# Decoder step on one core: gates computed in pairs of blocks with seven products, kept in DRAM

## The chip, the cores and the metric

The kernel runs on one core of a Trainium2 chip. The metric is the time of one execution on the device in microseconds; a time given for a kernel is the median of several executions. TensorE is called PE, VectorE DVE, ScalarE ACT, GpSimd POOL and SyncE SP. SP computes nothing here; it issues most of the DMAs, in a fixed order.

## What is computed

One layer of a hybrid decoder, for 1024 prompt positions and 8 sample rows, 1032 columns in all, everything in fp32. A projection of the input feeds three branches (window attention, a diagonal state-space layer with GELU and GLU, and a spatial gating over chunks of 128 positions) and, for every branch, a gate per output channel:

```python
q, k, v, z_a, u_b, z_b, u_c, v_c, z_c, g = jnp.split(x @ w_in, cuts, axis=-1)
y_a, y_b, y_c = attention(q, k, v), glu(gelu(s5(u_b))), sgu(u_c, v_c)
ys = stack([y_a * silu(z_a), y_b * silu(z_b), y_c * silu(z_c)])    # 512 wide each
branch = einsum('ntbw,bwd->ntbd', ys, w_read)                      # to 1024, per branch
gates = sigmoid(g.reshape(n, t, 3, 1024))
merged = (gates * branch).sum(axis=2)
x = layernorm(ALPHA * x + merged @ w_o, ln_g, ln_b)
```

The gate projection, 1024 input channels to 3 x 1024 gate channels, is the largest single product. It is made in 24 blocks of 128 output channels, 8 for each branch.

## The kernel before

Everything is held transposed: channels on the 128 partitions, the 1032 columns along the free axis, in three chunks of 344 (`CW`). An fp32 product is made of three: each operand is split into a high part, rounded to a shorter format, and the remainder, and `mm3` (L98) adds high by high (L101), high by low (L102) and low by high (L103) in PSUM. A piece of 128 x 128 weights by 344 columns thus takes three matmuls, each with a weight load of its own.

Weights come in granules of 128 x 512 (`gran`, L136): a DMA on SP into a raw tile `wr` (4 buffers), the high part `wh` by ACT (L133), the low part `wl` by a subtraction (L134), on DVE in the first part of the program and on POOL from L812 on. A block of the input projection has 8 pieces of 128 input channels in two granules, hence 72 matmuls: 8 x 3 for each of three chunks. A readout block has 4 pieces in one granule and 36 matmuls.

The instruction order on each engine is set by a scheduler that simulates the program when it is built; `tc.high_priority()` lets a step go ahead, `pin` and `behind` fix an order. PSUM is given out in banks: three of the kind `mm`, four `ms`, one `mt`. Large SBUF tiles (`b2`, 128 x 2064, named `b` in the trace) are 21.

The stages behind the state-space layer:

- Attention in 8 blocks (`attn_block`, L743): scores, softmax on DVE and ACT, transposes of the probabilities (L788) and the output matmuls (L794). Its end (L799 to L803) multiplies by the gate path z and splits the result into `yah` and `yal`, in SBUF. The twelve projections of the gating branch (L814 to L829) are interleaved with it.
- `readout(b, ...)` (L837) for the branches b = 0, 1, 2, with eight blocks d each. For each it first projects the gate block with 72 matmuls on the columns of x, takes a tanh on ACT (L846), then makes the readout product with 36 matmuls. DVE multiplies it by the gate (L856 for b = 0, L859 else). For b = 1 POOL adds it to the sum (L861); for b = 2 DVE adds it (L863) and the sum is split for the output projection (L866 on ACT, L867 on DVE).
- GELU of the state-space result (L885) runs in four steps between the blocks of readout 0; its split stays in SBUF. GLU follows (four blocks of 36 matmuls). The spatial gating (`sgu_chunk`, L977; LayerNorm in L938 to L946, the gating itself at L990 to L993) runs between the blocks of readout 1. Its result goes through DRAM (`ycD`) and is read back and split (L1004 and L1005) before readout 2.
- The output projection and the LayerNorm close the program.

Of the kernel before, what the change touches and what calls it, by code (L numbers as in the profile page):

```python
# [11 lines left out]
F32 = mybir.dt.float32  # L12
# [4 lines left out]
OP = mybir.AluOpType  # L17
# [47 lines left out]
def decoder_step(ctx, tc, io):  # L65
# [65 lines left out]
    def split_w(src, hi, lo):  # L131
        with tc.high_priority():
            S.activation(hi, src, AF.Copy)  # L133
            lo_eng[0].tensor_tensor(lo, src, f(hi), op=OP.subtract)  # L134

    def gran(idx, pinned=False):  # L136
        raw = wp.tile([128, 512], F32, tag="wr", name=nm("wr"), bufs=4)
        i1 = nc.sync.dma_start(raw, io["wg"][idx])
        if pinned:
            behind(i1, xlast[0])  # L140
        hi = wp.tile([128, 512], F32R, tag="wh", name=nm("wh"), bufs=4)
        lo = wp.tile([128, 512], F32R, tag="wl", name=nm("wl"), bufs=4)
        split_w(raw, hi, lo)
        return hi, lo
# [24 lines left out]
    wz = cst.tile([128, 512], BF16, name="wz")  # L169
    V.memset(wz, 0.0)  # L170
# [3 lines left out]
    prm = b2()  # L174
# [206 lines left out]
    qD, zaD, zbD, uszD, vcD, ycD, pD = (spill(n_) for n_ in ("qD", "zaD", "zbD", "uszD", "vcD", "ycD", "pD"))  # L381
# [293 lines left out]
    yah = [b2(F32R) for _ in range(2)]  # L675
    yal = [b2(F32R) for _ in range(2)]

# [46 lines left out]
    for j in range(2):  # L724
        h3 = v2(yah[j][:, 0:2 * T], T)[:, :, 0:NS]
        V.tensor_copy(h3, ysm3[:, 2 * j:2 * j + 2])
        V.tensor_tensor(v2(yal[j][:, 0:2 * T], T)[:, :, 0:NS], ysm3[:, 2 * j:2 * j + 2], f(h3), op=OP.subtract)
# [15 lines left out]
    def attn_block(m):  # L743
# [52 lines left out]
        y3 = z4  # L796
        for j in range(2):
            js = slice(2 * j, 2 * j + 2)
            V.scalar_tensor_tensor(y3[:, js], v2(o, 128)[:, js], 0.5, z4[:, js],  # L799
                                   op0=OP.mult, op1=OP.mult)  # L800
            h3 = v2(yah[j][:, 0:2 * T], T)[:, :, q0:q0 + 128]
            S.activation(h3, y3[:, js], AF.Copy)  # L802
            V.tensor_tensor(v2(yal[j][:, 0:2 * T], T)[:, :, q0:q0 + 128], y3[:, js], f(h3), op=OP.subtract)  # L803
# [29 lines left out]

    macc = [b2() for _ in range(4)]
# [43 lines left out]
    def gelu_load(q):  # L878
        wa = wks[q % 2][:, 0:T]
        i1 = nc.sync.dma_start(v2(wa[:, NS:T], 256), ytd[q])  # L880
        if q == 0:
            pin(i1)
# [318 lines left out]
```

## Time and profile before

| | |
|---|---|
| median of 3 runs | 997.93 us (997.4 to 998.44) |
| the profiled execution | 1001.31 us |
| its span (first to last instruction) | 999.2 us |
| mean granted clock of PE | 0.995 of full |
| DMA | 103.40 MB, mean 103 GB/s |

The profile's page comes from one execution, which was 3.4 us longer than the median; 2.1 us of it lie outside the span. An engine's busy time is the union of its instructions' spans. A line such as `L103 PE MATMUL mm<-b,wl 128*128 128x344` is a group: line 103, a matmul with 128 x 128 weights and 344 columns into a bank `mm`, from an SBUF tile and a low weight part. In groups the last columns are busy time and mean duration (ns), and the idle time of the engine just before them with what ended it. PEclk is the granted clock as a share of full speed.

### The profile page before, as it was taken

The page shows a single profiled execution, that of the slowest core. Times are in us where ns is not written, and L with a number is a line of the kernel's source. Part 1 is how long each engine was busy: PE and PEld are TensorE (multiplying, and loading weights), DVE is VectorE, ACT ScalarE, POOL GpSimd, SP SyncE. Part 2 cuts the span into 40 slices and gives each one's busy share as a digit, 9 for nine tenths or more (in the row PEclk, how much of TensorE's full clock was granted, in tenths as well). Part 3 has the DMA queues.
Part 4 walks back from the last instruction along what each step waited for, and adds up shares of the span by engine and source line. Part 5 has one row for each costly group of instructions (what it writes and reads, how often), then busy time and mean ns, then how long its engine had stood idle before and what let it go on. Part 6 is the DMA issues. An engine that isn't in the chain of part 4 may idle for free.

```text
span 999.2 us, 15902 instructions
## 1 busy us (share of the span) xinstructions
PE 984.8 (99%) x6105; PEld 929.1 (93%) x6105; DVE 558.2 (56%) x1218; ACT 336.0 (34%) x764; POOL 210.4 (21%) x194
## 2 busy tenths in 40 slices
PE   9999999999999999998999999999999999999997
PEld 7999999999999988885999999999999999986886
DVE  5877599999966664453434125145531323245754
ACT  5312464434324555455424134111122222241000
POOL 0420000001311212111222222434543222201411
PEclk9999999999999999998999999999999999999999
DMA  8445624443434222221433323233342111043311
GB/s 298 141 146 121 179 62 106 116 134 100 130 103 138 71 81 88 72 69 41 127 99 106 114 96 110 76 105 106 106 138 53 44 44 52 11 186 111 123 69 64
DMA packets 95772, 103.40 MB, mean 103 GB/s; under 512 B 36536, under 2 KB 70968, under 8 KB 94672
## 3 DMA queue, kind: packets, MB, share of 16 engines
q1 hardware_dynamic: 91184, 96.04, 32.2%
q10 hardware_dynamic: 4512, 6.34, 2.1%
q8 instruction: 48, 0.79, 0.3%
q14 instruction: 28, 0.23, 0.1%
HBM read 75.74 MB, written 26.29 MB: 102 GB/s over the span
## 4 chain that ended last, share of the span: by engine, by line
PE 92%; DVE 5%; DMA 1%; ACT 1%; issue 1%; SPq 0%; DVEq 0%; ACTq 0%
PE mm L101 26%; PE mm L103 26%; PE mm L102 26%; PE ms L794 2%; DVE b L254 2%; PE mt L788 1%; PE ms L102 1%; PE ms L767 1%; PE ms L103 1%; PE ms L101 1%; DMA b<-qD 1%; PE ms L1040 1%; PE ms L990 1%; PE ms L768 1%; DMA b<-xT 1%
## 5 line engine op out<-in xcount | busy, mean ns | idle before, releaser
L101 PE MATMUL mm<-b,wh 128*128 128x344 f32 x1584 | 508.4, 321 | 1.0 <-ACT b L802 1.0
L102 PE MATMUL mm<-b,wh 128*128 128x344 f32 x1584 | 507.0, 320 | 0.0
L103 PE MATMUL mm<-b,wl 128*128 128x344 f32 x1584 | 506.8, 320 | 0.0
L103 PEld LDWEIGHTS mm<-b,wl 128*128 128x128 f32 x1584 | 297.5, 188 | 3.7 <-issue 3.6
L101 PEld LDWEIGHTS mm<-b,wh 128*128 128x128 f32 x1584 | 297.5, 188 | 3.4 <-ACT b L802 2.4
L102 PEld LDWEIGHTS mm<-b,wh 128*128 128x128 f32 x1584 | 297.8, 188 | 1.7 <-issue 1.6
L134 POOL TENSOR_TENSOR wl<-wr,wh 128x512 fp32r<-128x512 f32 x100 | 138.9, 1392 | 592.5 <-ACT wh L133 554.9
L133 ACT ACTIVATE wh<-wr 128x512 fp32r<-128x512 f32 x136 | 85.6, 630 | 168.2 <-PE mm L102 129.1
L859 DVE SCALAR_TENSOR_TENSOR ct<-ct,mm 128x344 f32<-128x344 f32 x48 | 24.5, 510 | 123.7 <-PE mm L103 86.5
L846 ACT ACTIVATE ct<-mm 128x344 f32<-128x344 f32 x72 | 32.5, 451 | 116.8 <-PE mm L103 111.2
L254 DVE TENSOR_TENSOR b<-b 128x512 f32<-128x512 f32 (+6 forms) x93 | 53.9, 586 | 0.9
L101 PE MATMUL mm<-b,b 128*128 128x512 f32 (+1 forms) x136 | 51.9, 385 | 0.0
L102 PE MATMUL mm<-b,b 128*128 128x512 f32 (+1 forms) x136 | 51.4, 381 | 0.0
L103 PE MATMUL mm<-b,b 128*128 128x512 f32 (+1 forms) x136 | 51.4, 381 | 0.0
L856 DVE SCALAR_TENSOR_TENSOR b<-ct,mm 128x344 f32<-128x344 f32 x24 | 12.1, 511 | 64.7 <-PE mm L103 64.7
L254 DVE TENSOR_TENSOR b<-b,b 128x512 f32<-128x512 f32 (+5 forms) x96 | 44.8, 502 | 0.9
L771 DVE CUSTOM_DVE_ANT_0 b<-ms,b,sink 128x256 f32<-128x256 f32 (+1 forms) x64 | 26.2, 464 | 26.6 <-PE ms L768 26.5
L101 PEld LDWEIGHTS mm<-b,b 128*128 128x128 f32 x136 | 25.5, 188 | 7.5 <-ACT b L1045 0.8
L778 ACT ACTIVATE b<-b,stat 128x256 f32<-128x256 f32 (+1 forms) x64 | 30.9, 485 | 3.0 <-DVE stat L774 2.9
L134 DVE TENSOR_TENSOR wl<-wr,wh 128x512 fp32r<-128x512 f32 x36 | 24.6, 686 | 12.0 <-ACT wh L133 11.9
L102 PEld LDWEIGHTS mm<-b,b 128*128 128x128 f32 x136 | 25.5, 188 | 6.0 <-issue 0.8
L789 ACT ACTIVATE b<-mt 128x512 f32<-128x512 f32 x30 | 17.8, 593 | 39.0 <-PE mt L788 38.8
(233 smaller groups left out, 1087.4 us busy)
## 6 DMA issues: line engine op xcount, KB each, us to landing
wr<-wg SPq DMA_DIRECT2D x136, 256.0 KB, 2.9
b<-wo SPq DMA_DIRECT2D x4, 1024.0 KB, 9.0
b<-xp SPq DMA_DIRECT2D x8, 512.0 KB, 3.7
b<-xT SPq DMA_DIRECT2D x7, 516.0 KB, 6.7
yp<-b ACTq DMA_DIRECT2D x7, 512.0 KB, 2.6
zct<-b SPq DMA_DIRECT2D x5, 512.0 KB, 5.4
b<-zct SPq DMA_DIRECT2D x32, 80.0 KB, 2.6
utd<-b SPq DMA_DIRECT2D x4, 544.0 KB, 3.8
```

What stands on the lines that cost most here:

```text
L101: PE.matmul(out, ah, bh, start=start and i == 0, stop=False)
L102: PE.matmul(out, ah, bl, start=False, stop=False)
L103: PE.matmul(out, al, bh, start=False, stop=stop and i == n - 1)
L133: S.activation(hi, src, AF.Copy)
L134: lo_eng[0].tensor_tensor(lo, src, f(hi), op=OP.subtract)
L254: (eng or V).tensor_tensor(out, a, b, op=op)
L771: V.tensor_tensor_reduce(sc[:, h, lo:], p3[:, u, lo:], al3[:, h, lo:], SCALE, sink[:, h:h + 1], OP.add, OP.max, mx[:, h:h + 1])
L778: S.activation(sc[:, h, lo:], sc[:, h, lo:], AF.Exp, bias=nmx[:, h:h + 1], accum_out=den[:, h:h + 1])
L789: S.activation(pt[:, g, kb], tps, AF.Copy)
L794: PE.matmul(o[64 * g:64 * g + 64, :], vtok[:, m - 1 + kb, 64 * g:64 * g + 64], pt[:, g, kb], start=kb == kbs[0], stop=kb == kbs[-1])
L846: S.activation(tg, gps[c][:, :CW], AF.Tanh, scale=0.5)
L859: V.scalar_tensor_tensor(tt, tgs[c], 1.0, ps[:, :CW], op0=OP.add, op1=OP.mult)
```

## The change

The gate projection leaves the readouts. All 24 blocks are made in one stretch between the attention's last steps and GLU, their tanh is written to DRAM (`gD`), and a readout reads the gates of two blocks back with one DMA of 1 MB.

Two blocks (`gate_std`) are made as before, with 72 matmuls of 344 columns. The other 22 are made in 11 pairs (`gate_pair`). For a pair the weights are seen as a 2 x 2 matrix of granules (two output blocks by two halves of the input channels), and x as a 2 x 2 matrix of quarters (two halves of the input channels by two halves of the columns, 516 each). Eight products of such blocks would give the pair; Winograd's form of Strassen's scheme gives it with seven products of sums and differences. A product is made in two column pieces of 258 (`QT`), 4 x 3 matmuls each, hence 7 x 2 x 12 = 168 matmuls a pair. The four sums of x are made once, on POOL, and split on ACT and DVE; the four sums of weights are made for each pair on POOL; the products are added up on DVE (L919), which takes 14 additions of 128 x 258 a pair, seven `add` calls of two pieces. High and low parts of half of the weights are kept in columns of the split x that no product uses any more (`strips`).

Moved with it: the attention writes its result to `yaD` and no longer splits it; GELU writes its result to `y2D`; GELU and the spatial gating run between the pairs; `y_split` reads the three branch results back (L1043) and splits them on ACT and DVE just before GLU, readout 0 and readout 2. The tile for the first, idle matmuls lies in the parameter tile. There are five raw weight buffers in place of four.

```diff
-        y3 = z4
-        for j in range(2):
...
-            S.activation(h3, y3[:, js], AF.Copy)
-            V.tensor_tensor(v2(yal[j][:, 0:2 * T], T)[:, :, q0:q0 + 128], y3[:, js], f(h3), op=OP.subtract)
+        V.scalar_tensor_tensor(z4, v2(o, 128), 0.5, z4, op0=OP.mult, op1=OP.mult)
+        nc.sync.dma_start(yaD[:, :, q0:q0 + 128], z4)
...
+    def gate_std(i):
+        def go(c, ps):
+            tg = ct()
+            S.activation(tg, ps[:, :CW], AF.Tanh, scale=0.5)
+            nc.sync.dma_start(gD[i][:, cols[c]], tg)
+        proj(GG + i, go)
...
+        TT(f11, f12, f11, OP.subtract, G)
+        TT(f12, f22, f12, OP.subtract, G)
+        TT(f22, f22, f11, OP.subtract, G)
+        TT(f21, f21, f22, OP.subtract, G)
...
+            S.activation(h_[:, o], t_[:, o], AF.Copy)
+            TT(l_[:, o], t_[:, o], f(h_[:, o]), OP.subtract)
...
+        a11, a21 = wraw(i11)[0], wraw(i21)[0]
+        s3 = wraw()
+        TT(s3, a11, a21, OP.subtract, G)
...
+        def prod(w, n_):
+            ps = [bank()[:, :QT], bank(pk)[:, :QT]]
+            for c in range(2):
+                mm3(ps[c], [(w[0][:, k * 128:(k + 1) * 128], w[1][:, k * 128:(k + 1) * 128]) + bop(n_, k, c)
+                            for k in range(4)])
+            return ps
...
+        def add(o, a, b):
+            for c in range(2):
+                with tc.high_priority():
+                    V.tensor_tensor(o[c], a[c], b[c], op=OP.add)
...
+        ps = prod(w11, (0, 0))
...
+        add(u2, p1, prod(w2, 2))
+        add(c11, p1, prod(whl(a12, G), (1, 0)))
+        outs(0, 0, c11)
+        add(u3, u2, prod(whl(s3, V), 3))
+        ps = prod(whl(s1, V), 1)
+        add(p1, u3, ps)
+        outs(1, 1, p1)
+        add(u2, u2, ps)
+        add(u3, u3, prod(whl(a22, G), 4))
+        outs(1, 0, u3)
+        add(u2, u2, prod(whl(s4, V), (1, 1)))
+        outs(0, 1, u2)
...
+    todo = []
+    for q in range(4):
+        todo += [(gelu_step, q), (sgu_step, 2 * q), (sgu_step, 2 * q + 1)]
+    for n_ in range(NPR):
+        if n_:
+            gate_pair(NSTD + 2 * n_)
+        for fn, a_ in todo[12 * n_ // (NPR - 2):12 * (n_ + 1) // (NPR - 2)]:
+            fn(a_)
+    y2 = [y_split(y2D, j) for j in range(2)]
...
-            gg = [gran((GG + b * 8 + d) * 2), gran((GG + b * 8 + d) * 2 + 1)]
             gr = gran(GR_READ + b * 8 + d)
-            gps = [bank() for _ in range(NCH)]
-            tgs = []
-            for c in range(NCH):
-                proj_mm({c: gps[c]}, gg, [c])
-                tg = ct()
-                S.activation(tg, gps[c][:, :CW], AF.Tanh, scale=0.5)
-                tgs.append(tg)
+            if d % 2 == 0:
+                gt = b2()
+                nc.sync.dma_start(v2(gt[:, 0:2 * T], T), gD[b * 8 + d:b * 8 + d + 2].rearrange("d p t -> p d t"))
+            tgs = [gt[:, (d % 2) * T + c * CW:(d % 2) * T + (c + 1) * CW] for c in range(NCH)]
...
+    ya = [y_split(yaD, j) for j in range(2)]
+    readout(0, [y[0] for y in ya], [y[1] for y in ya])
+    readout(1, ybh, ybl)
+    yc = [y_split(ycD, j) for j in range(2)]
+    readout(2, [y[0] for y in yc], [y[1] for y in yc])
```

How the order of instructions changes is shown at three places; names carry the buffer's numbers, and "x4" stands for four instructions in a row.

PE at the end of the attention, before: from the last projection matmul (into `mm547`) to the first of readout 0 (into `mm548`), L788 transposes and L794 output matmuls of the last blocks.

```order
L103 MATMUL mm547_5146<-b308_3075,wl539_5048 128x344
L794 MATMUL ms379_3775<-b318_3132,b196_2140 64x512
L788 MATMUL mt382_3817<-ident_75,b317_3131 128x128 x4
L788 MATMUL mt383_3823<-ident_75,b317_3131 128x128 x4
L794 MATMUL ms388_3868<-b318_3132,b196_2140 64x512
L788 MATMUL mt386_3856<-ident_75,b317_3131 128x128 x4
L788 MATMUL mt387_3862<-ident_75,b317_3131 128x128 x4
L794 MATMUL ms388_3868<-b318_3132,b196_2140 64x512 x3
L101 MATMUL mm548_5160<-b307_3074,wh538_5047 128x344
```

The same place now: the last standard gate block (344 columns), then the first pair (258 columns, `mm563` and `mm565`), with the transposes (L792 now) and output matmuls (L798 now) of the last attention block further apart. First the switch from the standard block to the pair:

```order
L102 MATMUL mm543_5170<-b31_160,wh537_5110 128x344
L103 MATMUL mm543_5170<-b30_159,wl538_5111 128x344
L792 MATMUL mt379_3790<-ident_75,b313_3126 128x128 x4
L798 MATMUL ms384_3835<-b314_3127,b196_2142 64x512
L101 MATMUL mm563_5260<-b12_108 128x258
L102 MATMUL mm563_5260<-b13_109,b12_108 128x258
L101 MATMUL ms564_5261<-b12_108 128x258
L102 MATMUL ms564_5261<-b13_109,b12_108 128x258
```

The pair begins while the last attention block is still in its softmax. Fifteen rows further on, in the same product of the pair:

```order
L102 MATMUL mm563_5260<-b13_109,b12_108 128x258
L103 MATMUL mm563_5260<-b12_108,b13_109 128x258
L792 MATMUL mt382_3823<-ident_75,b313_3126 128x128 x4
L101 MATMUL mm563_5260<-b18_129,b12_108 128x258
L102 MATMUL mm563_5260<-b19_130,b12_108 128x258
L103 MATMUL mm563_5260<-b18_129,b13_109 128x258
```

So a group of transposes stands among matmuls that use only x, its sums and gate weights.

SP, in front of readout 0. Before, it holds weight loads there (`wr` from `wg`, L138 in `gran`) and the loads for GLU (`pD`), as between GELU and GLU here:

```order
L138 DMA wr679_6218<-wg 128x512
L138 DMA wr689_6280<-wg 128x512
L138 DMA wr698_6341<-wg 128x512
L913 DMA b682_6224<-pD_658 128x1032 x2
L138 DMA wr708_6403<-wg 128x512
L138 DMA wr724_6503<-wg 128x512
L138 DMA wr727_6509<-wg 128x512
```

Now, from the last of the gates' writes (L914) on: L1082 is a load for GLU, L1043 reads the attention's result back, L1104 reads gates back.

```order
L914 DMA gD_660<-b553_5238 128x258 x2
L1082 DMA b924_8409<-pD_659 128x1032 x2
L134 DMA wr983_8792<-wg 128x512
L134 DMA wr989_8840<-wg 128x512
L1043 DMA b944_8530<-yaD_656 128x2064
L134 DMA wr996_8890<-wg 128x512
L1043 DMA b947_8538<-yaD_656 128x2064
L134 DMA wr1002_8938<-wg 128x512
L1104 DMA b953_8552<-gD_660 128x2x1032
L1104 DMA b966_8650<-gD_660 128x2x1032
L134 DMA wr1012_8994<-wg 128x512
```

The reads of the attention's result and of the first gates stand behind weight loads of GLU and readout 0, each of which needs a free raw buffer.

DVE with a chunk of the spatial gating, before, in readout 1: LayerNorm (L941 to L946) and gating (L992, L993), between gate products (L859).

```order
L992 TENSOR_TENSOR b720_6471<-ms771_6833,b717_6464 128x512
L940 BN_STATS s6794_6995<-ms793_6990 128x6
L993 TENSOR_TENSOR b720_6471<-b720_6471 128x512
L941 BN_AGGR s6794_6995<-s6794_6995 128x2
L944 TENSOR_SCALAR b721_6472<-ms793_6990,s6794_6995 128x512
L945 TENSOR_TENSOR b721_6472<-b721_6472,b717_6464 128x512
L946 TENSOR_TENSOR b721_6472<-b721_6472,b717_6464 128x512
```

Now, in a pair: the same steps are L985 to L991, L1036 and L1037; between them stand the pair's additions from PSUM (L919) and weight splits (L146).

```order
L986 BN_AGGR s6618_5798<-s6618_5798 128x2
L919 TENSOR_TENSOR b553_5238<-b553_5238,mm631_5865 128x258
L989 TENSOR_SCALAR b584_5491<-mt617_5793,s6618_5798 128x512
L146 TENSOR_TENSOR b19_130<-wr654_6110,b18_129 128x512
L919 TENSOR_TENSOR b553_5238<-b553_5238,ms632_5866 128x258
L990 TENSOR_TENSOR b584_5491<-b584_5491,b582_5489 128x512
L919 TENSOR_TENSOR b553_5238<-b553_5238,mm633_5895 128x258
L991 TENSOR_TENSOR b584_5491<-b584_5491,b582_5489 128x512
L919 TENSOR_TENSOR b553_5238<-b553_5238,ms634_5896 128x258
L146 TENSOR_TENSOR b13_109<-wr652_6105,b12_108 128x512
L919 TENSOR_TENSOR b553_5238<-b553_5238,mm637_5931 128x258
L1036 TENSOR_TENSOR b584_5491<-mt619_5806,b582_5489 128x512
```

L989 uses what POOL computes from the result of L986, as L944 did before.

## Rows read from the trace of the kernel before

**Rows 1.** Page: busy time of PE and its weight loads; the chain by engine.

```profile
PE 984.8 (99%) x6105; PEld 929.1 (93%) x6105; DVE 558.2 (56%) x1218; ACT 336.0 (34%) x764; POOL 210.4 (21%) x194
...
PE 92%; DVE 5%; DMA 1%; ACT 1%; issue 1%; SPq 0%; DVEq 0%; ACTq 0%
```

**Rows 2.** Windows: start:end, length, busy us (instructions) of PE, PEld, DVE, ACT, POOL; PEclk, DMA, GB/s.

```profile
470.00:770.00 300.00, 300.00 (x1939) 299.62 (x1938) 111.50 (x161) 81.68 (x142) 101.93 (x93) 1.00 0.34 101
770.00:894.00 124.00, 124.00 (x791) 124.00 (x790) 40.08 (x72) 34.27 (x68) 25.93 (x20) 1.00 0.18 56
```

**Rows 3.** Timeline of PE: start, duration (us), instruction; 33 matmuls of 344 columns.

```profile
699.84 0.32 PE L103 MATMUL mm<-b,wl 128*128 128x344 f32 x1
...
704.86 0.32 PE L102 MATMUL mm<-b,wh 128*128 128x344 f32 x1
```

**Rows 4.** Timeline of PE: first and last of five starts (264 columns), of eight (256).

```profile
265.17 0.28 PE L103 MATMUL ms<-b,b 128*128 128x264 f32 x1
...
265.65 0.32 PE L102 MATMUL mm<-b,wh 128*128 128x344 f32 x1
...
443.82 0.28 PE L767 MATMUL ms<-b,b 128*128 128x256 f32 x1
...
444.66 0.28 PE L768 MATMUL ms<-b,b 128*128 128x256 f32 x1
```

**Rows 5.** Windows at the end of the attention, columns as in rows 2.

```profile
455.00:470.00 15.00, 11.69 (x42) 5.76 (x42) 4.40 (x13) 6.49 (x11) 0.00 (x0) 0.77 0.04 15
460.00:465.00 5.00, 4.31 (x13) 1.96 (x13) 0.00 (x0) 1.20 (x2) 0.00 (x0) 0.50 0.00 0
```

**Rows 6.** Timeline of PE at the end of the attention; last brackets: idle before, and its releaser.

```profile
445.74 0.60 PE L788 MATMUL mt<-ident,b 128*128 128x128 f32 x4
...
446.34 0.32 PE L102 MATMUL mm<-b,wh 128*128 128x344 f32 x1
...
450.33 1.08 PE L794 MATMUL ms<-b,b 128*64 128x512 f32 x4
451.34 0.42 PE L103 MATMUL mm<-b,wl 128*128 128x344 f32 x1
...
454.75 0.32 PE L103 MATMUL mm<-b,wl 128*128 128x344 f32 x1
...
467.65 0.58 PE L101 MATMUL mm<-b,wh 128*128 128x344 f32 x2 [0.96 <-ACT b L802]
```

**Rows 7.** Groups by line: form, count | busy us, mean ns | idle before, releasers.

```profile
L134 POOL TENSOR_TENSOR wl<-wr,wh 128x512 fp32r<-128x512 f32 x100 | 138.9, 1392 | 592.5 <-ACT wh L133 554.9 <-PE mm L103 28.2 <-PE mm L102 8.8
...
L861 POOL TENSOR_TENSOR b<-b,ct 128x344 f32<-128x344 f32 x24 | 25.6, 1071 | 9.6 <-DVE ct L859 9.6
...
L134 DVE TENSOR_TENSOR wl<-wr,wh 128x512 fp32r<-128x512 f32 x36 | 24.6, 686 | 12.0 <-ACT wh L133 11.9
L859 DVE SCALAR_TENSOR_TENSOR ct<-ct,mm 128x344 f32<-128x344 f32 x48 | 24.5, 510 | 123.7 <-PE mm L103 86.5 <-POOL wl L134 35.7 <-POOL b L861 1.3
...
L863 DVE TENSOR_TENSOR ct<-b,ct 128x344 f32<-128x344 f32 x24 | 18.9, 787 | 0.4
...
L799 DVE SCALAR_TENSOR_TENSOR b<-ms,b 128x256 f32<-128x256 f32 x16 | 6.0, 420 | 21.0 <-PE ms L794 21.0
...
L133 ACT ACTIVATE wh<-wr 128x512 fp32r<-128x512 f32 x136 | 85.6, 630 | 168.2 <-PE mm L102 129.1 <-issue 17.1 <-DMA wr<-wg 5.3
```

**Rows 8.** One line's instructions: shortest, median, longest (ns); first and last start.

```profile
L946 DVE TENSOR_TENSOR b<-b,b x9: 679/691/1766, 622.0 to 721.8; 128x512 f32<-128x512 f32 x8, 8x512 f32<-8x512 f32 x1
...
L863 DVE TENSOR_TENSOR ct<-b,ct x24: 508/517/1604, 772.8 to 898.8; 128x344 f32<-128x344 f32 x24
```

**Rows 9.** A DMA of 1 MB (KB each, us to landing); the split of one branch result.

```profile
b<-ycD SPq DMA_DIRECT2D x2, 1032.0 KB, 7.1
...
L1004 ACT ACTIVATE b<-b x4: 1049/1052/1067, 735.7 to 740.0; 128x1032 fp32r<-128x1032 f32 x4
...
L1005 DVE TENSOR_TENSOR b<-b,b 128x1032 fp32r<-128x1032 f32 x4 | 6.4, 1650 | 9.3 <-ACT b L1004 9.3
```

More of the change, by code (lines that the diff above doesn't have):

```diff
@@ L166, in proj @@
                 consume(c, ps)
-    wz = cst.tile([128, 512], BF16, name="wz")
-    V.memset(wz, 0.0)
+    prm = b2()
+    V.memset(prm[:, 1800:2056], 0.0)
+    wz = prm[:, 1800:2056].bitcast(BF16)
     wps = bank(pk)
@@ new lines, in decoder_step @@
+    tps = bank("t")
+    vs8 = uyt[0][:, 1024:1024 + 32]
+    behind(nc.sync.dma_start(v2(vs8, NS), vcD[:, :, 0:NS]), mark[1])
+    for g in range(4):
+        PE.transpose(tps[0:NS, g * 128:(g + 1) * 128], vs8[:, g * NS:(g + 1) * NS], ident)
+    vns = uyt[0][0:NS, 0:512]
+    sgu_norm(NS, tps, vns)
+    nc.sync.dma_start(io["vns"], vns)
+    tps = bank("t")
+    for g in range(4):
+        PE.transpose(tps[:, g * NS:(g + 1) * NS], vns[:, g * 128:(g + 1) * 128], ident[0:NS, 0:NS])
+    yc8 = uyt[0][:, 512:544]
@@ new lines, in sgu_chunk @@
+    def sgu_chunk(c):
+        t0_ = NS + c * 128
+        ub_ = uyt[(c + 1) % 2]
+        vt, us, vc_ = (ub_[:, n * 512:(n + 1) * 512] for n in range(3))
+        tps = bank("t")
+        for g in range(4):
+            i1 = PE.transpose(tps[:, g * 128:(g + 1) * 128], vc_[:, g * 128:(g + 1) * 128], ident)
+            if g == 0:
+                pin(i1)
+        sgu_norm(128, tps, vt)
+        ps = bank("t")
+        for g in range(4):
+            gs = slice(g * 128, (g + 1) * 128)
+            PE.matmul(ps[:, gs], vt[:, gs], wsm[:, gs], start=True, stop=True)
+        yc = vt
+        V.tensor_tensor(yc, ps, bsb, op=OP.add)
+        V.tensor_tensor(yc, yc, us, op=OP.mult)
+        nc.sync.dma_start(ycD[:, :, t0_:t0_ + 128], v2(yc, 128))
@@ new lines, in y_split, with gelu_step @@
+    def y_split(src, j):
+        yf, h_, l_ = b2(), b2(F32R), b2(F32R)
+        nc.sync.dma_start(v2(yf[:, 0:2 * T], T), src[:, 2 * j:2 * j + 2])
+        for e in range(2):
+            o = slice(e * T, (e + 1) * T)
+            S.activation(h_[:, o], yf[:, o], AF.Copy)
+            V.tensor_tensor(l_[:, o], yf[:, o], f(h_[:, o]), op=OP.subtract)
+        return h_, l_
+    gelu_load(0)
+    sgu_load(0)
+    sgu_load(1)
+    NPR = (24 - NSTD) // 2
+    def gelu_step(q):
+        gelu(q)
+        if q < 3:
+            gelu_load(q + 1)
@@ new lines, in sgu_step @@
+    def sgu_step(c):
+        sgu_chunk(c)
+        if c + 2 < NBLK:
+            sgu_load(c + 2)
+    todo = []
[7 more added lines that the diff above has]
+    y2 = [y_split(y2D, j) for j in range(2)]
+    y2h, y2l = [y[0] for y in y2], [y[1] for y in y2]
+    V.tensor_scalar(gb, gb, 0.5, None, op0=OP.mult)
```

293 lines of the change are left out of this document (143 added, 150 removed).

## The prediction, made before the changed kernel ran

> **What bounds the kernel now.** I read the page's busy times first: TensorE (PE) is busy 984.8 of 999.2 us and holds 92% of the chain that ended last [rows 1]. Then a table by stage, because that average could hide a stage with another limit: from 470 to 894 us, through GELU, GLU and the three readouts, PE is busy in every microsecond, while VectorE (DVE) and POOL each work little over a third of the time [rows 2]. So in this stretch only two things move the end: how many matmuls PE issues at what pace, and whatever new makes PE wait.
>
> Matmuls overlap, so their own 320 ns say little; the pace is the distance of two starts. Thirty-three matmuls of 344 columns start from 699.84 to 704.86, 32 steps of 0.157 us [rows 3]. Five starts of which the first four are of 264 columns lie from 265.17 to 265.65, 4 steps of 0.120; eight of 256 columns from 443.82 to 444.66, 7 steps of 0.120 [rows 4]. Each of them loads its own weights, as in the changed kernel.
>
> The one place with loose time is the end of the attention. Between the last projection matmul at 454.75 and the first matmul of readout 0 at 467.65 only the last attention block is left on PE: 16 transposes and 10 output matmuls. At the pace just before, four transposes took about 0.44 us (445.74 to 446.34, less one step of 0.157) and four output matmuls 1.01 [rows 6], so 4.3 us of work fill 12.7. PE idles 3.3 us of 15 there, and after it had waited its granted clock stood at 0.50 of full, the 1.2 GHz level, through 460 to 465 [rows 5]. Lost: 12.7 - 4.3 = 8.4 us.
>
> **The change, part by part.**
>
> 1. *Gates.* Twenty-two blocks of 72 matmuls of 344 columns go: 1,584 x 0.157 = 248.7 us. Eleven pairs of 7 products x 24 matmuls of 258 columns come: 1,848 x 0.120 = 221.8. PE is the bound there, so all of it counts: **-26.9 us**. The columns fall by an eighth, but matmuls rise by 264 in number, and each has a part that does not shrink with its columns; that eats some of the eighth. The size 258 is not in the trace. Its nearest rows are 256 and 264, both 0.120, and I take that. From the slope between 264 and 344 columns it would be 0.117; the rounding of the four steps allows 0.122. The term lies between -32.5 and -23.2.
>    The Trainium skill (TensorE: Matmul & The Clock Gate, Back-to-back issue gap) gives an isolated gap of columns/2.4 + 2.5 ns. By it the new matmuls would cost 110 ns each, 203 us in all; for 344 columns it gives 146 ns where the row has 157, so the measured steps decide.
>
> 2. *End of the attention.* The last two standard gate blocks and the first pair now stand between the steps of the last blocks, as the order of PE shows, and no readout matmul waits there for the attention's result any more. But ScalarE (ACT) and DVE now also split sixteen 516-wide pieces of the combined x inside that same chain: 16 x about 0.69 us on DVE (the 512-wide split [rows 7]) is 11 us, between the softmax steps for which PE's transposes wait. POOL's sixteen sums come earlier and lie behind projections. I keep 3 of the 8.4 us as a remaining wait: **-5.4**, between 0 and -8.4.
>
> 3. *Work on the other engines in the pairs.* One pair takes PE 168 x 0.120 = 20.2 us. DVE has 14 additions from PSUM, priced by the 256-wide operation that reads PSUM at 0.42: 5.9 us, and four weight splits at 0.69: 2.8 [rows 7]. GELU and the spatial gating move into this stretch. All that DVE does from 470 to 770 is 111.5 us [rows 2]; 48 readout products at 0.51 [rows 7] are 24.5 of it, so at most 87 us remain, 7.9 a pair. Sum 16.6 of 20.2. POOL has four weight sums and three splits, all 512 wide, at 1.39 [rows 7]: 9.7. ACT has seven splits and ten short copies or tanhs; all priced as a split, 0.63 [rows 7], that is under 11. All are covered, DVE with the least to spare.
>    That margin is not clean: the two-input DVE operations normally take 0.69 and 0.52, yet single ones took 1.77 and 1.60 [rows 8], about one POOL operation longer. The Trainium skill (SBUF — State Buffer, Who interferes with whom) says that a DVE instruction with two SBUF inputs and a POOL instruction that reads SBUF lock each other out whole; the trace agrees by those 1.1 us. A pair has about eight such DVE operations; were one in four blocked, as the mean of 787 against 517 ns in readout 2 suggests [rows 7, 8], DVE stands at 18.8 us. PSUM has three and four banks for the two halves of a product, so an addition may come some 5 us late before PE feels it. The two pairs that hold a GELU and a gating chunk at once may still exceed that: **+3**, between 0 and +10. The additions sit in DVE's order behind gating steps that wait for POOL; that is where it would show first.
>    The weights' DMAs stand on SP among eight gate writes a pair, each of which waits for its tanh; the splits run almost a pair ahead in DVE's order, so I charge nothing.
>
> 4. *From GLU to readout 0.* Readout 0 needs the attention's output and the first gates back from DRAM. The load of the gates for d = 0, 1 stands on SP behind a weight load whose buffer is freed only when the fourth readout weight is split, and that split waits for a weight buffer which GLU's last matmul holds. So it is issued about 2.4 us after GLU ends (0.63 for the split on ACT, 1.39 on POOL, the issue), and 1 MB lands in 7.1 us [rows 7, 9]: 9.5. Then DVE's first product, 0.5, frees the first of only three banks, at 10.1. PE has had work for three chunks of 12 x 0.157, 5.6 us. **+4.5**. The second half of the attention's output arrives in the same time (a load behind the previous weight, then 1.05 us on ACT and about 1.65 on DVE a half [rows 9]) and adds nothing of its own. Ends: 0, if 1 MB lands in 3 us; +9, if both loads share the engines and take 12.
>
> 5. *The rest, at nothing.* The reload of the GELU result happens two products before the last pair ends; if it were late it would be felt at GLU's first matmul. Writing the attention's output to DRAM replaces its split and leaves ACT lighter. The warm-up tile in the parameter tile only moves a memset before the first x has landed. Twelve gate loads of 1 MB come one per 11.3 us of readout. Readout 1 puts POOL at 3 x 1.07 + 1.39 = 4.6 of 5.65 us a block (1.07 is its 344-wide addition); readout 2 puts DVE at 0.51 + 0.52 + 0.51 = 1.54 of 1.88 us a chunk, or 1.81 with the mean of the middle one [rows 7, 8]. Before, the gate matmuls gave three times that cover. It holds, narrowly; if it does not, see the rivals. The output projection keeps its order.
>
> **Sum:** -26.9 - 5.4 + 3 + 4.5 = -24.8 us. The profiled execution took 1001.31 us with a span of 999.2, the median of the runs is 997.93. From the span that is 974.4, and from the median **973.1 us**, which I forecast.
>
> **The rivals.**
>
> *DVE becomes the bound in places.* If half of the two-input operations are blocked by POOL, and the waits of the gating steps come on top, the nine pairs with extra work take some 21.5 us in place of 20.2: +12, and readout 2 at 1.88 + 0.2 a chunk adds 5: about 987. For it: the single long rows and the narrow margins of parts 3 and 5. Against: the medians are the short values even where POOL was busy a third of the time.
>
> *The boundaries cost more.* Each new trip through DRAM could stand in full, 7.1 + 2.1 + 3.3 us, before GLU as well as before readout 0: about 12.5 and 4.5 more than charged, some 988. Against: the order puts the first one well ahead.
>
> *The other side: PE's pace is that of its weight loads.* The loads are busy 929.1 us, 93% of the span, and one lasts 188 ns, longer than the step of a 344-column matmul [rows 1, 3]. If they set the pace, 258 columns cost 0.157 as well, and the pairs 1,848 x 0.157 = 290.1 us: 41 more than the gates before, so 973 + 68 = 1041. It decides from a step of about 0.133 us on, where the pairs have lost all that the other terms leave. The Trainium skill (Perfetto Trace Analysis, Identifying the Most-Contended Engine) indeed judges a matmul kernel by the busy share of its loads, and by that the extra 264 loads would be paid in full. Against: matmuls of 256 and 264 columns step at 0.120 with one load each [rows 4], so the loads overlap.
>
> That the seven products do not replace eight can be ruled out: the order has 168 matmuls a pair.
>
> **How the numbers follow.** Forecast as summed 0.72, DVE in places 0.14, boundaries 0.07, pace of the loads 0.03, and 0.04 for a stall that I have not found. About 0.2% (2 us) is what a measurement tells from no change. Faster by more than that: 0.92; within it: 0.03; slower: 0.05. With the ends of parts 1 to 4 not all on one side at once, the forecast's own range is 963 to 981; taking in the first two rivals up to their centres the range is **961 to 988**.
>
> **What would show it.** Right: 258-column matmuls that start 0.117 to 0.122 us apart; PE busy in all of the pairs but a few us; idle time of 2 to 9 us on PE just behind GLU, ended by DVE's first readout product or the split of the attention's output; no half-clock stretch at the attention's end. Wrong: steps of 0.13 or more; PE waiting on L919 (the additions) in most pairs; PE waiting for DVE in readout 2 chunk after chunk; an idle PE of over 5 us at the end of the attention.

## The result and the profile after

The changed kernel takes 986.77 us (median of 4 runs, 985.78 to 988.04), the kernel before, on the same chip, 998.18: a ratio of 0.9886, 95% interval 0.9869 to 0.9903. That is 11.4 us faster, where 24.8 were forecast. The profiled execution has a span of 986.2 us, 13.0 less than the 999.2 of before. All that follows is counted on the spans; they differ by 1.6 us more than the medians do, since the profiled execution of before was 3.1 us above its median and this one 1.3.

The page's busy times:

```profile
PE 962.7 (98%) x6369; PEld 906.5 (92%) x6369; DVE 657.7 (67%) x1408; ACT 372.9 (38%) x845; POOL 276.7 (28%) x243
```

PE has 264 matmuls more and is busy 22.1 us less than before [rows 1]. A table of stages shows where it is not busy: the end of the attention, the pairs, GLU with the readouts, and single stretches of 10 us (columns as in rows 2):

```profile
448.40:466.80 18.40, 18.40 (x108) 15.39 (x107) 15.97 (x38) 16.16 (x41) 3.57 (x3) 1.00 0.19 63
...
466.80:717.40 250.60, 241.13 (x1968) 237.83 (x1968) 154.58 (x282) 104.93 (x206) 111.72 (x94) 0.99 0.58 175
717.40:881.60 164.20, 161.65 (x1011) 160.28 (x1012) 85.48 (x154) 47.85 (x86) 57.73 (x48) 0.99 0.47 170
540.00:550.00 10.00, 5.75 (x48) 5.56 (x47) 4.60 (x8) 1.31 (x3) 5.77 (x6) 0.93 0.34 94
550.00:560.00 10.00, 10.00 (x64) 10.00 (x65) 7.41 (x15) 3.75 (x8) 4.43 (x3) 0.73 0.46 135
740.00:750.00 10.00, 7.45 (x35) 6.56 (x34) 7.16 (x9) 4.61 (x9) 1.62 (x1) 0.83 0.74 282
```

The attention's end has no idle time and no lower clock any more [rows 5]. In the pairs PE is idle 9.5 us of 250.6, while DVE works 62% of the stretch and POOL 45%: neither is full. The waits of PE from 466 to 780 us (waiter, what it waited for, total, times, longest):

```profile
PE mt L1034 <- DVE b L991: 8.1, 5, 4.2
PE mm L101 <- ACT b L1046: 2.0, 1, 2.0
PE mt L1004 <- DVE b L991: 1.4, 1, 1.4
PE mm L102 <- DVE b L1047: 0.5, 1, 0.5
```

L1004 and L1034 are not the pairs' matmuls. They belong to the spatial gating (L1004 are transposes of its eight sample rows, L1034 a chunk's gating matmuls) and wait for the last step of its LayerNorm on DVE (L991). L1046 and L1047 are the split of the attention's result in front of readout 0. The timeline of PE has the longest wait, the pace of the new matmuls, and the waits behind GLU:

```profile
549.88 2.05 PE L1034 MATMUL mt<-b,b 128*128 128x128 f32 x8 [4.25 <-DVE b L991]
...
700.04 0.28 PE L101 MATMUL mm<-b,wh 128*128 128x258 f32 x1
...
703.99 0.28 PE L101 MATMUL mm<-b,b 128*128 128x258 f32 x1
...
745.37 0.74 PE L101 MATMUL mm<-b,wh 128*128 128x344 f32 x3 [2.02 <-ACT b L1046]
...
746.63 0.65 PE L102 MATMUL mm<-b,wh 128*128 128x344 f32 x1 [0.53 <-DVE b L1047]
```

From 700.04 to 703.99 lie 34 starts, 33 steps of 0.120 us: the pace is what the prediction took.

**The longest wait, followed back.** On DVE, the LayerNorm of that chunk:

```profile
537.27 0.69 DVE L985 BATCH_NORM_STATS2 s<-mt 128x6 f32<-128x512 f32 x1
537.99 0.18 DVE L986 BATCH_NORM_AGGREGATE s<-s 128x2 f32<-128x6 f32 x1
545.40 0.81 DVE L989 TENSOR_SCALAR b<-mt,s 128x512 f32<-128x512 f32 x1 [7.23 <-POOL s L988]
...
548.00 1.74 DVE L991 TENSOR_TENSOR b<-b,b 128x512 f32<-128x512 f32 x1
```

DVE stood still for 7.23 us until POOL's second tiny step (L988, 128 x 1) was done. On POOL, meanwhile:

```profile
536.09 1.75 POOL L146 TENSOR_TENSOR b<-wr,b 128x512 fp32r<-128x512 f32 x1
540.78 1.29 POOL L263 TENSOR_TENSOR wr<-wr,wr 128x512 f32<-128x512 f32 x1 [2.94 <-DMA wr<-wg]
542.03 1.30 POOL L146 TENSOR_TENSOR b<-wr,b 128x512 fp32r<-128x512 f32 x1
543.29 1.30 POOL L263 TENSOR_TENSOR wr<-wr,wr 128x512 f32<-128x512 f32 x1
544.54 0.19 POOL L987 TENSOR_TENSOR s<-s,mh 128x1 f32<-128x1 f32 x1
544.81 0.56 POOL L988 TENSOR_TENSOR s<-s,mh 128x1 f32<-128x1 f32 x1
```

The tiny steps, 0.75 us of work, were ready at 538.2 and stood behind a weight sum (L263) that waited for a weight from DRAM, then a split (L146), then another sum. Before, a chunk's steps went through at once, here on DVE:

```profile
668.92 0.17 DVE L941 BATCH_NORM_AGGREGATE s<-s 128x2 f32<-128x6 f32 x1
670.03 0.81 DVE L944 TENSOR_SCALAR b<-ms,s 128x512 f32<-128x512 f32 x1 [0.93 <-POOL s L943]
```

From the end of the aggregate to the end of POOL's second step it took 0.9 to 2.1 us in the eight chunks of before, and 0.9 to 8.2 us now. The whole chain from a chunk's transposes to the end of its LayerNorm took 5.4 to 6.9 us before, and PE had 53 to 58 matmuls of 0.157 us in front of the gating matmuls, 8.3 to 9.1 us. Now it takes 6.7 to 14.4, and PE has 69 to 94 matmuls of 0.120, 8.3 to 11.3 us.

So there was a theory after the first look: a chain DVE, POOL, DVE that is now longer than the work that covers it. Its rivals were a DVE that is too full or locked by POOL, and loads that come late and would reach PE on any way.

### The profile page after: what moved, and what is told of

Its sections match the earlier page's. It is cut to its first block, busy times and chain, and to the rows that moved or that the text cites. A ratio compares the mean times of both kernels' runs of the same rounds, so it can differ in the third digit from the quotient of the medians.

```text
span 986.2 us, 17101 instructions
## 1 busy us (share of the span) xinstructions
PE 962.7 (98%) x6369; PEld 906.5 (92%) x6369; DVE 657.7 (67%) x1408; ACT 372.9 (38%) x845; POOL 276.7 (28%) x243
## 5 line engine op out<-in xcount | busy, mean ns | idle before, releaser
L101 PE MATMUL mm<-b,wh 128*128 128x344 f32 (+1 forms) x1208 | 382.8, 317 | 2.0 <-ACT b L1046 2.0
L102 PE MATMUL mm<-b,wh 128*128 128x344 f32 (+1 forms) x1208 | 383.2, 317 | 0.5 <-DVE b L1047 0.5
L103 PE MATMUL mm<-b,wl 128*128 128x344 f32 (+1 forms) x1208 | 382.7, 317 | 0.0
L101 PEld LDWEIGHTS mm<-b,wh 128*128 128x128 f32 x1208 | 227.8, 189 | 4.3 <-ACT b L1046 2.3
L102 PEld LDWEIGHTS mm<-b,wh 128*128 128x128 f32 x1208 | 228.3, 189 | 3.5 <-issue 2.4
L103 PEld LDWEIGHTS mm<-b,wl 128*128 128x128 f32 x1208 | 228.1, 189 | 2.9 <-issue 2.8
L146 POOL TENSOR_TENSOR wl<-wr,wh 128x512 fp32r<-128x512 f32 x72 | 103.1, 1433 | 409.5 <-ACT wh L145 392.1
L102 PE MATMUL mm<-b,b 128*128 128x258 f32 (+2 forms) x292 | 96.1, 330 | 0.0
L103 PE MATMUL mm<-b,b 128*128 128x258 f32 (+2 forms) x292 | 96.1, 330 | 0.0
L101 PE MATMUL mm<-b,b 128*128 128x258 f32 (+2 forms) x280 | 92.6, 333 | 0.0
L263 POOL TENSOR_TENSOR wr<-wr,wr 128x512 f32<-128x512 f32 x44 | 59.5, 1353 | 61.2 <-DMA wr<-wg 34.5
L102 PEld LDWEIGHTS mm<-b,b 128*128 128x128 f32 x292 | 55.3, 189 | 6.9 <-DVE b L1125 0.8
L103 PEld LDWEIGHTS mm<-b,b 128*128 128x128 f32 x292 | 55.2, 189 | 5.9 <-issue 0.8
L101 PEld LDWEIGHTS mm<-b,b 128*128 128x128 f32 x280 | 53.0, 189 | 6.1 <-ACT b L1161 0.8
L146 DVE TENSOR_TENSOR wl<-wr,wh 128x512 fp32r<-128x512 f32 x58 | 44.8, 774 | 20.6 <-ACT wh L145 20.4
L263 DVE TENSOR_TENSOR b<-b,b 128x512 f32<-128x512 f32 (+6 forms) x112 | 55.0, 527 | 0.9
L102 PE MATMUL ms<-b,b 128*128 128x258 f32 (+1 forms) x188 | 54.2, 288 | 1.2 <-DVE b L557 1.2
L263 DVE TENSOR_TENSOR b<-b 128x512 f32<-128x512 f32 (+6 forms) x93 | 53.6, 583 | 0.9
L103 PE MATMUL ms<-b,b 128*128 128x258 f32 (+1 forms) x172 | 49.3, 287 | 0.0
```

The source lines that it names most:

```text
L101: PE.matmul(out, ah, bh, start=start and i == 0, stop=False)
L102: PE.matmul(out, ah, bl, start=False, stop=False)
L103: PE.matmul(out, al, bh, start=False, stop=stop and i == n - 1)
L146: (eng or lo_eng[0]).tensor_tensor(lo, raw, f(hi), op=OP.subtract)
L263: (eng or V).tensor_tensor(out, a, b, op=op)
```

## Experiments

All are changes of the changed kernel, each timed against the kernel before on the same chip; sums and differences below are between medians. The kernel before had 997.9 to 998.2 us in all of them.

### The chain without POOL

```diff
-        V.tensor_scalar(vn, ps[0:rows, :], s6[0:rows, 6:7], s6[0:rows, 9:10], op0=OP.subtract, op1=OP.mult)
+        V.tensor_scalar(vn, ps[0:rows, :], s6[0:rows, 6:7], mh[0:rows, 0:1], op0=OP.subtract, op1=OP.mult)
```

> The changed kernel, but the normalisation in the spatial gating multiplies by a constant in place of the reciprocal deviation; POOL still computes that (L987, L988), and nothing waits for it. So one part of the LayerNorm is left out. Theory (POOL's queue): the 9.5 us that PE waits in front of the gating matmuls (L1004, L1034) come from two tiny POOL steps that stand behind weight sums, which wait for weights. Then the idle time there falls to under 2 us, the half-clock stretch near 550 us goes, and the time is about 975 us (973 to 978). Rival (DVE too full, or locked by POOL): the steps L989 to L991 are late anyway, idle time there stays over 6 us and the time is 984 to 987. Second rival (the weights themselves are late): the wait moves to the pairs' own matmuls, 982 or more.

Measured: 983.42 us (ratio 0.9858, 0.9841 to 0.9874), a gain of 3.4 where the theory said 12. PE's waits in the pairs:

```profile
PE mt L1034 <- DVE b L991: 3.5, 2, 1.8
PE mt L1027 <- DVE b L1036: 2.8, 1, 2.8
```

The wait for L991 fell from 9.5 us to 3.5, as the theory wants. The rival of a full DVE does not get its 6 us at this place either. But the run does not decide, since the order changed with the edit: the gating matmuls of most chunks now stand 51 matmuls behind their transposes, in place of 69 to 94, and a new wait appeared in front of the next transposes (L1027).

### Gate writes issued by ACT

```diff
-            nc.sync.dma_start(gD[i + m][:, h * HT + c * QT:h * HT + (c + 1) * QT], t_)
+            nc.scalar.dma_start(gD[i + m][:, h * HT + c * QT:h * HT + (c + 1) * QT], t_)
```

> The changed kernel with the gates' DMA writes in the pairs issued by ACT in place of SP, so that no weight load stands behind a gate write on SP. Theory (POOL's queue, fed late): POOL's wait for weight DMAs in front of the weight sums (34.5 us in all) falls by more than half, and the idle time of PE in front of the gating matmuls from 9.5 to under 4 us: about 979 us (976 to 982). Rival (the loads are late because the raw buffers are freed late): POOL waits as long as before, 985 to 988. Rival (DVE too full): the waits for weights fall, the idle time of PE stays, 985 to 988.

Measured: 985.99 us (0.9875, 0.9861 to 0.989), no gain that is clear of the noise. POOL's wait for weights in front of its sums, from 466 to 720 us, is first the row of the changed kernel, then that of this one:

```profile
POOL wr L263 <- DMA wr<-wg: 34.5, 13, 4.4
```

```profile
POOL wr L263 <- DMA wr<-wg: 41.4, 14, 3.8
```

The loads are as late as before, so the gate writes on SP do not hold them. The first rival's time and wait came; whether its reason holds, that raw buffers come free late, is tested below.

### Reads for readout 0 ahead of GLU

```diff
     y2h, y2l = [y[0] for y in y2], [y[1] for y in y2]
+    gt0 = b2()
+    nc.sync.dma_start(v2(gt0[:, 0:2 * T], T), gD[0:2].rearrange("d p t -> p d t"))
+    ya = [y_split(yaD, j) for j in range(2)]
...
-            if d % 2 == 0:
+            if b == 0 and d == 0:
+                gt = gt0
+            elif d % 2 == 0:
...
-    ya = [y_split(yaD, j) for j in range(2)]
```

> The changed kernel with the first read of the gates and both reads and splits of the attention's result put ahead of GLU. Theory: the 2.55 us that PE waits behind GLU and the lower clock after it go: 986.8 - 5 = 982 us (981 to 984). Rival (the transfers and splits only move): they delay GLU's own loads or splits, PE waits in front of GLU, and the time is 985 to 988.

Measured: 982.65 us (0.9841, 0.9827 to 0.9856), 4.1 us gained, as the theory said. The waits for L1046 and L1047 are gone from PE's list; the gating's remain.

### All 24 blocks as full blocks

```diff
     for n_ in range(NPR):
-        if n_:
-            gate_pair(NSTD + 2 * n_)
+        gate_std(NSTD + 2 * n_)
+        gate_std(NSTD + 2 * n_ + 1)
```

The sums of x and all that belongs to the pairs are cut out.

> The changed kernel with all 24 gate blocks made as full blocks (72 matmuls of 344 columns) in the same stretch, gates through DRAM; no pairs, no sums of x or of weights, GELU and gating between the blocks as now. Theory (the loss belongs to the pairs' POOL sums): PE does not wait in front of the gating matmuls (under 1 us in all), the end of the attention gains some 4 to 5 us, the step from GLU to readout 0 costs about 5, so that the time is that of before: 998 us (995 to 1001). Rival (the loss belongs to the stretch, with GELU, gating and DRAM traffic next to each other): the gating waits stay and it takes 1005 or more.

Measured: 1000.99 us (1.003, 1.002 to 1.004), within the theory's range. PE's list from 466 to 780 us, where L936 is the gating matmul and L948, L949 the split in front of readout 0:

```profile
PE mm L101 <- ACT b L948: 2.0, 1, 2.0
PE mt L936 <- DVE b L893: 1.0, 1, 1.0
PE mm L102 <- DVE b L949: 0.5, 1, 0.5
```

So the stretch and the trips through DRAM cost 3 us without the pairs. That is net: PE has no idle time at the attention's end in this run either, so what was lost there before is given back. The gating hardly waits without the pairs; but with them POOL's weight sums, DVE's additions and the seven raw tiles a pair all went at once, so this run does not say which of them it is. What the pairs bring in place of full blocks is 1000.99 - 986.77 = 14.2 us, about half of the 26.9 that their matmuls save.

### Gating matmuls held back

The gating matmuls of a chunk become a step of their own, ordered behind the sixth product of the next pair (`behind` fixes an order and adds no wait):

```diff
+            i1 = PE.matmul(ps[:, gs], vt[:, gs], wsm[:, gs], start=True, stop=True)
+            if g == 0:
+                behind(i1, adds[-14 + AT])
```

> The changed kernel with the gating matmuls (L1034) of a chunk held back in PE's order until the sixth product of the next pair: 105 to 172 matmuls of the pair now stand between a chunk's transposes and its gating matmuls (31 for the last chunk of a merged couple), where 72 to 96 stood. Nothing else is changed. Theory (a chain of small steps through DVE, POOL and DVE that is longer than the PE work put in front of its matmul): the chain may stay as long as it is, up to 14.4 us, but PE has 12.6 to 20 us of work; its idle time in the pairs falls from 9.5 to under 1.5 us, no half-clock stretch is left there, and the time is 975 us (973 to 978). Rival (DVE, held up by L989 that waits for POOL, delays the pair's additions and splits as well): the idle time moves to the pair's own matmuls, 982 to 987.

Measured: 988.41 us (0.9894, 0.9863 to 0.9925), no gain. The first theory falls as it was put. PE no longer waits at L1034's place, and waits elsewhere:

```profile
PE mt L1027 <- issue: 5.8, 1, 5.8
PE mm L101 <- DVE b L919: 3.1, 1, 3.1
PE mt L1027 <- DVE b L1044: 1.5, 2, 1.3
```

The 5.8 us in its timeline, POOL, DVE and PE one after the other:

```profile
676.73 1.26 POOL L263 TENSOR_TENSOR wr<-wr,wr 128x512 f32<-128x512 f32 x1 [5.83 <-DMA wr<-wg]
...
680.53 0.55 POOL L988 TENSOR_TENSOR s<-s,mh 128x1 f32<-128x1 f32 x1
...
681.11 0.81 DVE L989 TENSOR_SCALAR b<-mt,s 128x512 f32<-128x512 f32 x1 [4.78 <-POOL s L988]
...
682.02 1.09 PE L1027 MATMUL mt<-ident,b 128*128 128x128 f32 x4 [5.76 <-issue]
```

It is the same chain: a sum on POOL waits 5.83 us for a weight, the tiny steps behind it are late, DVE's L989 is late. L989 reads the transposes from the only bank `mt`, and the next chunk's transposes start 0.1 us after it ends at 681.92. The 3.1 us are another way: there DVE waited 2.37 us for GELU's read from DRAM, and the additions behind it in its queue freed their banks late.

### Both edits that failed alone

The constant in the normalisation and the matmuls held back, as shown above.

> The changed kernel with both edits that failed alone: the normalisation multiplies by a constant (one part of the LayerNorm left out), so that no chain runs through POOL's tiny steps, and the gating matmuls are held back by 105 to 172 matmuls. Raw buffers, loads and everything behind GLU are as in the changed kernel. Theory (in the changed kernel, PE's waits in the pairs come by the chain through POOL; loads are late, but reach PE only that way): PE is idle for under 2 us in the pairs and the time is 974 to 978 us. Rival (late loads reach PE on other ways too, through DVE's queue or the weights): 3 us or more of idle time in the pairs, in front of the pairs' own matmuls or the transposes, 980 to 985.

Measured: 985.4 us (0.9875, 0.9859 to 0.9892). The rival's case: no chain through POOL, matmuls held back, and PE still waits 6.1 us in the pairs:

```profile
PE mt L1027 <- DVE b L1044: 3.2, 1, 3.2
PE mm L101 <- DVE b L919: 2.9, 3, 1.3
```

Most of this is another late load: in front of the waits at 562.54 and 666.64, 4.3 us together, DVE had stood still for 2.81 and 3.39 us until GELU's read from DRAM (L967) had landed, and L1044 or the pair's additions stood behind it in DVE's queue. DVE waits for that read in the changed kernel too, 7.9 us in all. So the chain through POOL is one way on which late loads reach PE in the changed kernel, DVE's queue is another, and cutting the first gained little: 3.4 us alone, 1.4 with the matmuls held back.

### Two sums in tiles of their own

A pair takes seven raw tiles (four loads and the sums s2, s3, s4; s1 is added in place) of five buffers. Here s3 and s4 get free columns of two other tiles, so that a pair takes five of five:

```diff
-        s3 = wraw()
+        s3 = lnp[:, 1536:2048]
...
-        s4 = wraw()
+        s4 = uyt[0][:, 1536:2048]
```

> The changed kernel with two of a pair's weight sums (s3, s4) in tiles of their own, so that a pair takes five of the five raw buffers in place of seven, and loads can run a whole pair ahead. Theory (the loads are late because raw buffers come free late, and POOL's queue passes this on): POOL's wait for weight DMAs in front of the weight sums falls from 34.5 to under 12 us, DVE's wait of 27.6 us for POOL's L988 at least halves, and the time is 978 to 982. Rival (gate writes on SP hold the loads, or the chain is long for DVE's own reasons): 985 to 988.

Measured: 981.79 us (0.9831, 0.9805 to 0.9857), 5.0 us gained, within the theory's range. DVE's waits for POOL's L988, first in the changed kernel, then here:

```profile
DVE b L989 <- POOL s L988: 27.6, 8, 7.2
```

```profile
DVE b L989 <- POOL s L988: 12.8, 8, 4.1
```

They halve, as expected, though this alone does not show the reason: with the gate writes on ACT they were 12.9 us as well, and nothing was gained. POOL's waits for weights fell less than I had written, from 34.5 to 28.1 us (24.6 in front of sums into the new tiles and 3.5 in front of the others). The gating's wait on PE fell from 9.5 to 5.6 us; part of that is scatter, since it was 7.7 with the early reads, which leave the order in the pairs as it was.

What shows the reason is when SP issues a pair's four loads. Here are those of the sixth pair, whose first matmul starts at 585.9 us in the changed kernel and at 581.6 with the new tiles; first the changed kernel, then this one (x2 stands for two loads in a row):

```profile
580.81 0.81 SPq L134 DMA_DIRECT2D wr<-wg  x2
...
584.05 0.33 SPq L134 DMA_DIRECT2D wr<-wg  x1
...
591.12 0.33 SPq L134 DMA_DIRECT2D wr<-wg  x1
```

```profile
565.25 0.43 SPq L134 DMA_DIRECT2D wr<-wg  x1
...
567.38 1.06 SPq L134 DMA_DIRECT2D wr<-wg  x2
...
581.37 0.33 SPq L134 DMA_DIRECT2D wr<-wg  x1
```

In the mean of the second to the eleventh pair the four loads start 7.2, 6.3 and 1.2 us ahead of the pair's first matmul and 6.1 us behind it in the changed kernel. With the new tiles it is 16.7, 13.8, 11.7 and 1.7 us ahead, so each comes 7 to 11 us earlier. With the gate writes on ACT the four numbers stay within 1.1 us of the changed kernel's. So it was the raw buffers that made the loads late. The edit is one of buffers alone, but the built order of instructions changes with it on every engine (a chunk's gating matmuls have 66 to 93 matmuls in front of them), so the 5.0 us need not all be due to the loads. It is the only single edit in the pairs that gained what it promised.

### The edits together

The edits are those shown above. Matmuls held back, with the early reads:

> The gating matmuls held back, and the reads of the first gates and of the attention's result put ahead of GLU. Theory: both gains add up, 975 - 4 = 971 us (969 to 974), and PE is idle for under 2 us between 470 and 880 us. Rival (each stall hides another one): 975 or more.

Measured: 982.41 us (0.9839, 0.9812 to 0.9866), what the early reads give alone. The rival holds.

With the two tiles as well:

> As the kernel before, and the two weight sums in tiles of their own. Theory: with the gating matmuls held back PE feels no late weight, so this changes nothing beyond 1 us: 971 us (968 to 974). Rival (late weights still cost PE something): 2 us or more below the kernel without these tiles.

Measured: **973.71 us** (0.9747, 0.9718 to 0.9776), 8.7 us below the kernel without the tiles: the rival again, late weights cost PE more than I had thought. It has the lowest median of all versions, 24.4 us below the kernel before and 13.1 below the changed one. PE's waits in the pairs:

```profile
PE mt L1027 <- issue: 1.9, 1, 1.9
PE mt L1027 <- DVE b L1044: 1.4, 1, 1.4
PE mt L1004 <- DVE b L991: 0.4, 1, 0.4
```

The tiles and the early reads, without holding back:

> The two weight sums in tiles of their own, and the reads of the first gates and of the attention's result ahead of GLU; the gating matmuls stand where the changed kernel has them, 70 to 97 matmuls behind their transposes. Theory (loads that come late, passed on from queue to queue, whatever stands at the end of the chain): holding the gating matmuls back gave nothing while loads were late, and gives something once they are early; so this one is 977 to 980 us, the sum of the two single gains (5.0 and 4.1 off 986.8), and 3 to 5 us slower than with the matmuls held back (973.7). Rival (the held-back matmuls never matter): 973 to 975.

Measured: 977.56 us (0.9796, 0.9779 to 0.9813), as the theory said: single gains add up, and holding the matmuls back is worth 3.9 us once the loads are early and nothing while they are late. How much it is worth is known only roughly: the next version, which holds them back too and issues the gate writes on ACT, lies only 2.2 us below this one, with intervals that overlap.

The fastest version with the gate writes on ACT:

> Sums in tiles of their own, early reads, gating matmuls held back, and in addition the gate writes of the pairs issued by ACT. Theory (SP's queue is the next thing that makes loads late once raw buffers are free): POOL's wait for weight loads falls from 25 to under 15 us, the last 3.3 us of idle time in front of transposes to under 1.5, and the time is 970 to 972.5 us. Rival (as with the gate writes moved alone: SP's place for them costs nothing): 973 to 975.

Measured: 975.41 us (0.9777, 0.9755 to 0.9799), not below the version without. POOL's wait for weights did not fall to under 15 us either; it rose, from 26 to 40. The place of the gate writes on SP is not the next limit. Two kernels whose runs spread over 4 us each are not told apart further.

The fastest version with POOL's order turned round:

```diff
-        TT(s3, a11, a21, OP.subtract, G)
+        i3 = G.tensor_tensor(s3, a11, a21, op=OP.subtract)
+        if pw:
+            behind(i3, pw[-1])
```

> Sums in tiles of their own, early reads, gating matmuls held back, and in addition POOL's order changed: the first weight sum of a pair stands behind the two tiny steps of the last chunk before it. Theory: DVE's wait for POOL's second tiny step falls from 12 to under 5 us, but PE no longer feels that chain, so the time stays at 973 to 975 us. Rival (the chain through POOL still costs PE time): 969 to 972. Other side (the sums come later and weights with them): 976 or more.

Measured: 1044.55 us (1.0465, 1.0443 to 1.0486), the other side and far beyond what I had put there. PE's waits:

```profile
PE mm L101 <- ACT b L145: 30.9, 5, 7.6
PE mm L101 <- ACT wh L145: 19.5, 3, 8.1
```

The first sum of a pair now stands behind the tiny steps of a chunk that runs only at the start of that same pair on PE. So the splits of the sums are not ready when PE wants them, and in six pairs it waits 7 to 8 us. Whichever stands first in POOL's queue makes the other late.

## Why the prediction was wrong

The direction was right, but of the 24.8 us forecast only 11.4 came. That the time lies inside the range, just under its upper end, is luck: two rivals had set that end, and neither is what happened. The terms, measured by the same counts (steps of 0.157 and 0.120 us, transposes and output matmuls as in the prediction):

- **Gates, -26.9: right.** The steps are 0.120 us; 264 more weight loads cost nothing more, so the rival on the pace of the loads is out. The measure of the Trainium skill (Perfetto Trace Analysis, Identifying the Most-Contended Engine), the busy share of the loads, is 92% here and did not tell what more loads cost: a load lasts 0.189 us and a step 0.120.
- **End of the attention, -5.4: right, -6.2.** The 18.4 us from 448.4 hold 86 matmuls of 344 columns, 12 transposes and 8 output matmuls, 16.8 us of work, and the first pair loses 0.8 more among the last transposes: 2.4 lost. By the same count the 19.4 us of before up to 467.6 lost 8.6 (32 matmuls, 20 transposes and 14 output matmuls are 10.8 us). The splits on ACT and DVE that I had kept 3 us for do not show as a wait. One reading was wrong, without effect on the sum: the matmuls at 454.75 and 467.65 are both of readout 0, the end of its second chunk and the start of its third. Its first gate block and two chunks of its first product stood ahead of the gap (DVE's products L856 start at 453.22 and 455.94), and the third waited for the attention's result.
- **The other engines in the pairs, +3: wrong, +13.** The 250.6 us hold 1,848 x 0.120 = 221.8 us of the pairs, 10.6 of the gating and 2.4 of the attention; 15.8 are lost, 0.8 of them counted above. The same work without pairs, 427.0 us from 467.6 before, lost 1.9. Of the 15, PE's idle time is 9.5; the half-clock stretch behind the longest wait is 2.7 (550 to 560 at 0.73 of full). By the distances of the starts, about 1 more goes with the last matmul in front of each wait, which runs its full 0.28, and about 2 are in steps that are 1% over 0.120 in the mean.
- **From GLU to readout 0, +4.5: right in size, +5.9 at most, by another way.** The gates were there in time. PE waited 2.5 us for the split of the attention's result, of which I had said that it adds nothing of its own, and the clock fell behind it. Reading both earlier gave back 4.1.
- **The rest, at nothing: right.** PE has no wait in the readouts behind that, and the middle operation of readout 2 (L1121) has a mean of 605 ns, below the 787 of before.

One more term, which the prediction had at nothing, lies ahead of the attention's end: up to 448.4 us PE has started six matmuls of 344 columns fewer than before up to 448.2, +1.1.

Sum: -26.9 - 6.2 + 13.1 + 5.9 + 1.1 = -13.0, as the spans differ.

The step that failed is in part 3, the +3 us for the other engines in the pairs, which came to +13.1: engines were priced by their busy time in a pair (DVE 16.6 of 20.2 us; by the trace 154.58 of 250.6, or 14.1 of 22.8 a pair), and the loads of weights were charged nothing because the splits run almost a pair ahead in DVE's order. Neither DVE nor POOL was full, and the split of a weight was never what PE waited for. What I had not counted is that a pair takes seven raw tiles from five buffers, so that loads start late, and that work of the spatial gating stands behind those loads in POOL's queue. I had named the place ("gating steps that wait for POOL"), but priced it as an addition that may come 5 us late, not as a chain of 14 us that ends in a matmul on PE's own queue. The Trainium skill (Perfetto Trace Analysis, Optimization Strategy) says that the same gap repeating on the engine that should be full can mean too little room for the next tile. The runs with two sums in tiles of their own agree, by 5.0 and 8.7 us.

The rival of DVE as the bound gave 987 us, almost the measured time, for another reason: its blocked operations are there (L991 ran from 548.00 for 1.74 us while POOL's split ran from 547.93 for 1.26, so some 1.1 of the longest wait's 4.25 us are this), but no stretch is bound by DVE, and making loads earlier, which takes no work from DVE, gave back 5.0 us alone and 8.7 in company. The rival of the boundaries is also mis-added: 973.1 + 12.5 + 4.5 is 990, not 988.

Open is why the steps in the pairs are a little over 0.120, and what GELU's late read costs by itself. The chain through POOL was never cut with the order left as it was: no run here has the reciprocal deviation on an engine other than POOL.

## What to carry to other kernels

Busy shares do not price a stretch in which several in-order queues feed each other: follow each short chain that ends in a matmul, count how long it takes with everything that stands in front of it on each queue, and compare it with the PE work that covers it. Before work with loads is put on an engine that also carries a few tiny, urgent steps, count its buffers per turn: seven tiles from five buffers made the loads late. When a wait is taken away and the time stays, look where the next one appeared: here the late thing was further back.

## What was not expected of the hardware

The clock after a wait: behind the 4.25 us of idle time at 549.88 the granted clock was 0.73 in the next 10 us (0.50, the 1.2 GHz level, from 550 to 553), and with the 2.55 us at 745 it was 0.83 from 740 to 750. Those 6.8 us of waits cost about 4 us more. But the kernel with the constant in the normalisation waits the same 2.0 and 0.5 us behind GLU, and up to 2.8 in the pairs, and in its profiled execution the clock was 1.00 in every stretch of 10 us from 470 to 800. It differs from one execution of that kernel to the next as well: the mean granted clock was 0.998 in this one, of 981.33 us, and 0.993 in its longest, of 984.62. So the price of one wait can't be read off its length alone, and what decides was not looked into.
